# Norms spread by two float32r products instead of one fp32 product, two levels of the gated attention computed block by block, and products of ones at the program's start

## The chip, the cores and the metric

One core of one Trainium2 chip runs the whole program in one launch. The metric is the device time of an execution in microseconds (us); lower is better. The engines are named as in the profile: PE (TensorE, with PEld for its weight loads), DVE (VectorE), ACT (ScalarE), POOL (GpSimd), SP (SyncE).

## The reference

A decoder trunk of two layers on 512 tokens with 16 learned tokens ahead of them, so 528 columns; the model width is 1024, all in float32.

```python
# layer i:  x += 0.5*SwiGLU_a(RMSNorm(x)); x += Mixer_i(RMSNorm(x)); x += 0.5*SwiGLU_b(RMSNorm(x))
def rmsnorm(x, g):  # x * rsqrt(mean(x*x) + 1e-6) * g
def swiglu(x, w_in, w_out):      # d_ff = 2816
    gate, up = split(x @ w_in); return (silu(gate) * up) @ w_out
# mixer of layer 0: retention, 4 heads (dk 256, dv 512), rotary positions, a decay per head,
#   RMSNorm per head, gated by silu(g), output product
# mixer of layer 1: gated linear attention (GLA), 4 heads (dk 128, dv 256), a decay per key channel
#   and token, in exact form inside a chunk, RMSNorm per head, gated, output product
# at the end: final RMSNorm; the 16 learned tokens are dropped
```

So there are seven norms over the model width (two FFNs and a mixer per layer, and the final one), and one norm per head in each mixer.

## The kernel before

Activations lie with the channels on the partitions and the tokens in the columns; x stays on the core. A large product is made of three float32r products (`mm3`, L361 to L363): activations and weights are split into a high float32r part and the rest (`whi` by ACT at L139, `wlo` by DVE at L140), and high by high, rest by high and high by rest are added up in PSUM. The FFNs combine such products over halves of the matrices (`pf10g`, `Xf20o` and so on).

The RMSNorm of a stage is made by `enter(gcol, by, lag)`. While the stage before writes x, `scaled` (ACT, DVE L434) makes the two parts of x times the gain, and `squared` (ACT, DVE L442) adds the squares of the eight row groups of x up in `sqa_n`. Then `stats` runs: 1-column fp32 products with a column of ones sum the squares over the partitions, each for a block of tokens, and leave token sums on partitions (`st_n`, PE L468); `ms_n` (DVE L477) makes the mean; POOL raises it to -1/2 into `rc` (L479); DVE multiplies the identity by it, which gives diagonal blocks (`dg_n`, L481). One step of the stage later (`later`) `spread` multiplies the diagonals by a matrix of ones in fp32, which puts each token's factor on all partitions (`bc_n`, PE L488), and ACT copies it to `rb` (L489). The blocks of tokens are given by `by`: `BY_P` is 16 columns and four blocks of 128, `BY_JT` the same with the 16 at the end (on 16 partitions).

`rsqrt_rows` (L392) does the same for the norms of heads and the final one: `st` L401, `ms` L404, POOL L406, diagonal `dg` L408, spread `bc` L414. A retention head has six blocks of 88 tokens and two spreads of 264 columns (`ro`), a GLA head one of 512 (`go`), the end one of 256 (`fa`). What is made from `bc_ro` is the gated output `og`, split into `ogh` and `ogl` (DVE L390), which the output projection `po_r` takes.

The GLA computes scores inside a chunk by levels (`levels`): at level s, each token in the second half of a group of 2s is scored against the keys of the first half. `tile_scores` (L1395) makes, for each of two passes over pairs of heads, eight fp32 products of 128 keys by 64 queries into `lv`; most of the results aren't wanted, and DVE's `copy_predicated` (L1425) takes the wanted ones into `Pd` by a mask of level s. `advance` then multiplies decays into Q and K. Between levels, `filler` gives PE a step of other products.

The engines run their instructions in an order that a scheduler works out from the program and from priorities: `urgent()` puts what is inside it 300 steps ahead. Before the first FFN product is over, `plain_first` runs 96 float32r products that need no norm yet. Temporary tiles are taken from rings by tag; `hf` is a ring of two, which `dg`, `og` and the `hf` of the FFN share.

```python
def rsqrt_rows(sq, parts, width, name, finish):     # L392
    ...
    dg = tmp.tile([P, T], F32, tag="hf", name=f"dg_{name}")                 # L407
    V.tensor_tensor(dg[:w, :n]..., ident[:w, :w]..., r[:w, :nj]..., ALU.mult)
    def spread(q):
        nc.tensor.matmul(bc[:, :np_], lhsT=ones[:w, :], rhs=dg[:w, q * np_:(q + 1) * np_], start=True, stop=True)
```

Of the kernel before, what the change touches and what calls it, by code (L numbers as in the profile page):

```python
# [10 lines left out]
F32 = mybir.dt.float32  # L11
# [26 lines left out]

NJ = 5
# [5 lines left out]
BY_P = ((16, 128, 4, 512), (0, 128, 1, 16))  # L45
PW = 512
AHEAD = 4
HEAD_START = 300
# [149 lines left out]
def trunk(ctx, tc, a):  # L198
# [125 lines left out]
    ones = const.tile([P, P], F32, name="ones")  # L324
    V.memset(ones, 1.0)
# [65 lines left out]

    def rsqrt_rows(sq, parts, width, name, finish):  # L392
# [7 lines left out]
        for j in range(nj):  # L400
# [6 lines left out]
        dg = tmp.tile([P, T], F32, tag="hf", name=f"dg_{name}")  # L407
        V.tensor_tensor(dg[:w, :n].rearrange("p (j t) -> p j t", j=nj),  # L408
                        ident[:w, :w].unsqueeze(1).broadcast_to([w, nj, w]),
                        r[:w, :nj].unsqueeze(2).broadcast_to([w, nj, w]), ALU.mult)  # L410

        def spread(q):
            bc = bank(f"bc_{name}{q}")
            nc.tensor.matmul(bc[:, :np_], lhsT=ones[:w, :], rhs=dg[:w, q * np_:(q + 1) * np_], start=True, stop=True)  # L414
            finish(bc, q)
# [3 lines left out]
    def enter(gcol, by, lag=1):  # L419
# [42 lines left out]
        def stats():  # L462
# [11 lines left out]
            dg = tmp.tile([P, T], F32, tag="hf", name=f"dg_{name}")  # L474
            for (b0, w, nb, m), c in zip(by, cols):
# [4 lines left out]
                n = m // nb  # L480
                V.tensor_tensor(dg[:w, b0:b0 + m].rearrange("p (j t) -> p j t", j=nb),  # L481
                                ident[:w, :n].unsqueeze(1).broadcast_to([w, nb, n]),
                                r.unsqueeze(2).broadcast_to([w, nb, n]), ALU.mult)
# [791 lines left out]
    def gla(feed):  # L1275
        with tc.tile_pool(name="glap", bufs=1) as gp, psum_pool(2) as pp:
            other["pool"] = pp
            masks = gp.tile([P, 7, HP], I32, tag="masks", name="masks")
# [101 lines left out]
            def levels(p, filler):  # L1380
# [18 lines left out]

                pd_v = Pd.rearrange("p h (J i) -> p (h J) i", i=P)  # L1400
# [22 lines left out]
                while s <= 64:  # L1423
                    ps = tile_scores(f"lv{p}_{s}", s)
# [239 lines left out]
    feed = enter(G_F1, BY_P, 4)  # L1664
# [7 lines left out]
    retention(enter(G_F2, BY_P))  # L1672
    ffn("f2", 0, HALVES, G_F2, enter(G_F1 + 8, BY_P))
# [5 lines left out]
def _constants():  # L1679
# [14 lines left out]
    lmask = [((j >> n) % 2 == 0) & ((i >> n) == (j >> n) + 1) for n in range(7)]  # L1694
# [62 lines left out]
```

## Time and profile before

| what | us |
|---|---|
| median of three runs (lowest to highest) | 2105.49 (2105.16 to 2106.26) |
| the profiled execution: device time | 2106.07 |
| the profiled execution: span of the core | 2104.3 |
| PE busy | 2078.2 (99% of the span) |
| DVE busy | 1761.3 (84%) |
| ACT busy | 1165.0 (55%) |
| POOL busy | 195.9 (9%) |

The device time of the profiled execution is 1.8 us above its span, and 0.58 us above the median. Busy time of PE says that it had something in its pipeline, not that it was at its peak: what an event costs on PE is read from the distance between the starts of products around it.

### The profile page before, as it was taken

The numbers are of one execution on the slowest core, as the hardware profiler recorded it, in microseconds if no ns is written. First come the engines' busy times: TensorE is split into PE (matmuls) and PEld (weight loads), VectorE is DVE, ScalarE is ACT, GpSimd is POOL, SyncE is SP. The second block draws the span as 40 slices with busy tenths as digits, with TensorE's granted clock in tenths as the row PEclk, the third lists the DMA queues.
The fourth block names the chain that finished last, engine by engine and source line by source line (L and its number), as shares of the span: only waits on it lengthen the run. The fifth ranks groups of instructions, "written<-read, shape, count | busy, mean of one in ns | idle before, by whom it ended". The sixth has DMA issues, their size and how long they took to land.

```text
span 2104.3 us, 43710 instructions
## 1 busy us (share of the span) xinstructions
PE 2078.2 (99%) x16842; PEld 2051.9 (98%) x16842; DVE 1761.3 (84%) x3139; ACT 1165.0 (55%) x2250; POOL 195.9 (9%) x168
## 2 busy tenths in 40 slices
PE   8999999999999999999999999999999999999998
PEld 8999999999999999999999999999999999999998
DVE  8989889978686779988889998888775659998886
ACT  5656666554545455656665565666632335666664
POOL 1011111010101000111110011111000000111110
PEclk9999999999999999999999999999999999999999
DMA  7576777254544532776776476676512122586772
GB/s 219 154 191 159 191 183 192 88 151 121 152 121 126 142 100 66 183 194 155 197 182 163 114 177 184 167 196 170 146 61 68 57 73 67 136 221 168 188 181 71
DMA packets 171809, 309.12 MB, mean 147 GB/s; under 512 B 17104, under 2 KB 40016, under 8 KB 171600
## 3 DMA queue, kind: packets, MB, share of 16 engines
q1 hardware_dynamic: 131696, 231.20, 32.8%
q0 software_dynamic: 38896, 71.84, 21.1%
q10 hardware_dynamic: 1008, 3.29, 0.5%
q8 instruction: 132, 2.16, 0.4%
q14 instruction: 77, 0.63, 0.1%
HBM read 304.16 MB, written 2.10 MB: 146 GB/s over the span
## 4 chain that ended last, share of the span: by engine, by line
PE 92%; DVE 3%; ACT 2%; issue 1%; DMA 1%; POOL 0%; SPq 0%; DVEq 0%; POOLq 0%; ACTq 0%
PE po_r L361 1%; PE po_r L362 1%; PE po_r L363 1%; PE lv L1395 1%; PE Xf11o L361 1%; PE Xf20o L361 1%; PE Xf11o L363 1%; PE Xf20o L363 1%; PE Xf11o L362 1%; PE Xf20o L362 1%; PE Xf10o L361 1%; PE Xf10o L363 1%; PE Xf10o L362 1%; PE Xf11u L361 1%; PE Xf21o L361 1%
## 5 line engine op out<-in xcount | busy, mean ns | idle before, releaser
L139 ACT CAST whi<-raw 128x512 fp32r<-128x512 f32 (+1 forms) x886 | 524.1, 606 | 544.3 <-DVE raw L145 73.4
L140 DVE TENSOR_TENSOR wlo<-raw,whi 128x512 fp32r<-128x512 f32 (+1 forms) x886 | 580.0, 669 | 174.7 <-ACT whi L139 165.8
L139 ACT CAST whi<-pair 128x512 fp32r<-128x512 f32 (+1 forms) x290 | 174.8, 603 | 129.1 <-DVE pair L145 8.1
L140 DVE TENSOR_TENSOR wlo<-pair,whi 128x512 fp32r<-128x512 f32 (+1 forms) x290 | 192.3, 663 | 8.4 <-ACT whi L139 7.2
L112 POOL DMA_DIRECT2D pair<-in_f_in x75 | 91.1, 1215 | 767.1 <-DVE wlo L140 379.1
L112 POOL DMA_DIRECT2D pair<-in_f_out x48 | 58.1, 1210 | 414.2 <-DVE wlo L140 209.3
L145 DVE TENSOR_TENSOR raw<-pair,raw 128x512 f32<-128x512 f32 (+1 forms) x139 | 92.5, 665 | 2.6
L147 DVE TENSOR_TENSOR raw<-raw,raw 128x512 f32<-128x512 f32 (+1 forms) x139 | 92.4, 665 | 2.6
L361 PE MATMUL po_r<-ogh,whi 128*128 128x264 f32 x256 | 72.8, 284 | 1.3 <-DVE xa L873 1.3
L362 PE MATMUL po_r<-ogl,whi 128*128 128x264 f32 x256 | 72.8, 284 | 0.0
L363 PE MATMUL po_r<-ogh,wlo 128*128 128x264 f32 x256 | 72.5, 283 | 0.0
L112 POOL DMA_DIRECT2D pair<-in_ret_in x20 | 24.3, 1216 | 300.3 <-DMA pair<-in_ret_in 131.5
L361 PE MATMUL Xf11o<-hf,whi 128*128 128x264 f32 x176 | 51.0, 290 | 0.9 <-ACT whi L139 0.6
L361 PE MATMUL Xf20o<-hf,whi 128*128 128x264 f32 x176 | 51.0, 290 | 0.9 <-ACT whi L139 0.6
L361 PE MATMUL Xf10o<-hf,whi 128*128 128x264 f32 x176 | 50.9, 289 | 0.9 <-ACT whi L139 0.6
L362 PE MATMUL Xf11o<-hf,whi 128*128 128x264 f32 x176 | 50.1, 285 | 0.0
L362 PE MATMUL Xf20o<-hf,whi 128*128 128x264 f32 x176 | 50.1, 284 | 0.0
L362 PE MATMUL Xf10o<-hf,whi 128*128 128x264 f32 x176 | 50.1, 284 | 0.0
L363 PE MATMUL Xf20o<-hf,wlo 128*128 128x264 f32 x176 | 49.9, 284 | 0.0
L363 PE MATMUL Xf11o<-hf,wlo 128*128 128x264 f32 x176 | 49.9, 284 | 0.0
L363 PE MATMUL Xf10o<-hf,wlo 128*128 128x264 f32 x176 | 49.9, 284 | 0.0
L361 PEld LDWEIGHTS po_r<-ogh,whi 128*128 128x128 f32 x256 | 48.1, 188 | 1.7 <-DVE xa L873 1.7
(834 smaller groups left out, 8663.0 us busy)
## 6 DMA issues: line engine op xcount, KB each, us to landing
raw<-in_f_in SPq DMA_DIRECT2D x277, 256.0 KB, 4.4
pair<-in_f_in SPq DMA_DIRECT2D x150, 256.0 KB, 4.5
pair<-in_f_in POOLq DMA_DIRECT2D x75, 512.0 KB, 6.1
raw<-in_f_out SPq DMA_DIRECT2D x80, 256.0 KB, 3.7
raw<-in_ret_in SPq DMA_DIRECT2D x76, 256.0 KB, 3.3
raw<-in_f_out SPq DMA_DIRECT2D x72, 192.0 KB, 3.0
raw<-in_gla_in SPq DMA_DIRECT2D x50, 256.0 KB, 2.8
pair<-in_f_out SPq DMA_DIRECT2D x48, 256.0 KB, 3.8
```

Of the source, the lines that this page charges most:

```text
L112: nc.gpsimd.dma_start(t, aps[2].unsqueeze(1).broadcast_to([P, 2, n]), accum_op=ALU.add)
L139: self.nc.scalar.copy(hi[:, :n], raw)
L140: V.tensor_sub(lo[:, :n], raw, hi[:, :n].bitcast(F32))
L145: V.tensor_add(s2, self.tiles[c][:, 1], self.tiles[c, "a11"])
L147: V.tensor_add(raw, raw, s2)
L361: nc.tensor.matmul(ps, lhsT=lh, rhs=rh, start=start, stop=False, **kw)
L362: nc.tensor.matmul(ps, lhsT=lh, rhs=rl, start=False, stop=False, **kw)
L363: nc.tensor.matmul(ps, lhsT=ll, rhs=rh, start=False, stop=stop, **kw)
L1395: nc.tensor.matmul(ps[:, j, J * P:J * P + n], lhsT=Kt[:, j, J * P:(J + 1) * P], rhs=q, start=(J == 0), stop=(J == 3), skip_group_check=True)
```

## The change

1. `diagonals` takes the factor apart into its float32r high part and the rest (two small DVE instructions, a CAST L411 and a subtraction L412) and makes two diagonals, `dgh` and `dgl` (L414), both in the ring `hf`. `spread_rows` (L420) adds up two float32r products with ones. It takes the place of the one fp32 product in `enter` and in `rsqrt_rows`.
2. In `enter` for the inputs of the first FFN (`G_F1`), of layer 0's second FFN (`G_F2`) and of layer 1's first FFN (`G_F1 + 8`) the blocks of tokens are `BY_6`: six blocks of 88 in one group, so one mean, one power and one diagonal instruction instead of two each, and the spread in two pieces of 264 columns. The inputs of the retention, of the GLA and of the last FFN keep blocks of 128.
3. GLA levels 32 and 64 are computed by `block_scores`: for each group of tokens and each tile, one product of s keys by s queries (16 of 32x32 at level 32, 8 of 64x64 at level 64, per pass), and ACT copies the results into `Pd`, two copies at level 32 and one at level 64. `copy_predicated` goes at these levels.
4. Ten float32r products of ones (`warm`, 128x512, L336) stand ahead of the first product, into a PSUM tile that isn't read.

```diff
-    ones = const.tile([P, P], F32, name="ones")
-    V.memset(ones, 1.0)
+    ones_r = const.tile([P, P], F32R, name="ones")
+    V.memset(ones_r.bitcast(F32), 1.0)
+    ones = ones_r.bitcast(F32)
+    warm = acc.tile([P, 2, 512], F32, tag="acc", name="warm")[:, 0, :]...
+    for _ in range(WARM):                                    # WARM = 10
+        nc.tensor.matmul(warm, lhsT=ones_r, rhs=ones_r.unsqueeze(1).broadcast_to([P, 4, P]), start=True, stop=True)
+    def parts_of(name):
+        return [tmp.tile([P, T], F32R, tag="hf", name=f"dg{i}_{name}") for i in "hl"]
+    def diagonals(dg, name, r, w, c0, n):
+        nj = r.shape[1]
+        m = n // nj
+        rr = tmp.tile([P, 2, 8], F32R, tag="rr", name=f"rr_{name}")
+        V.tensor_copy(rr[:w, 0, :nj], r)
+        V.tensor_sub(rr[:w, 1, :nj], r, rr[:w, 0, :nj].bitcast(F32))
+        for i, d in enumerate(dg):
+            V.tensor_tensor(d[:w, c0:c0 + n].rearrange("p (j t) -> p j t", j=nj),
+                            ident[:w, :m].unsqueeze(1).broadcast_to([w, nj, m]),
+                            rr[:w, i, :nj].bitcast(F32).unsqueeze(2).broadcast_to([w, nj, m]), ALU.mult)
+    def spread_rows(ps, dg, w, c0):
+        for i, d in enumerate(dg):
+            nc.tensor.matmul(ps, lhsT=ones_r[:w, :], rhs=d[:w, c0:c0 + ps.shape[1]], start=(i == 0), stop=(i == 1))
...
+BY_6 = ((0, 88, 6, 528),)
             def spread():
                 for b0, w, nb, m in by:
-                    bc = bank(f"bc_{name}_{b0}")
-                    nc.tensor.matmul(bc[:, :m], lhsT=ones[:w, :], rhs=dg[:w, b0:b0 + m], start=True, stop=True)
-                    S.copy(rb[:, b0:b0 + m], bc[:, :m])
+                    n = m if m <= 512 else m // 2
+                    for c0 in range(b0, b0 + m, n):
+                        bc = bank(f"bc_{name}_{c0}")
+                        spread_rows(bc[:, :n], dg, w, c0)
+                        S.copy(rb[:, c0:c0 + n], bc[:, :n])
...
+                def block_scores(name, s):
+                    ps = acc_tile(name)
+                    blocks = range(P // (2 * s))
+                    for j in range(2):
+                        for n in blocks:
+                            k0 = 2 * s * n
+                            for J in range(4):
+                                nc.tensor.matmul(ps[k0:k0 + s, j, J * P:J * P + s],
+                                                 lhsT=Kt[:, j, J * P + k0:J * P + k0 + s],
+                                                 rhs=Qt[:, j, J * P + k0 + s:J * P + k0 + 2 * s],
+                                                 start=(J == 0), stop=(J == 3), skip_group_check=True)
+                    for n in blocks:
+                        k0 = 2 * s * n
+                        S.copy(pd_v[k0:k0 + s, :, k0 + s:k0 + 2 * s],
+                               ps.rearrange("p h (J i) -> p (h J) i", i=P)[k0:k0 + s, :, :s])
...
                 while s <= 64:
+                    if s >= BLOCKS:                          # BLOCKS = 32
+                        block_scores(f"lv{p}_{s}", s)
+                        tot = advance(s, tot)
+                        filler()
+                        s *= 2
+                        continue
...
-    feed = enter(G_F1, BY_P, 4)
+    feed = enter(G_F1, BY_6, 4)
-    retention(enter(G_F2, BY_P))
-    ffn("f2", 0, HALVES, G_F2, enter(G_F1 + 8, BY_P))
+    retention(enter(G_F2, BY_6))
+    ffn("f2", 0, HALVES, G_F2, enter(G_F1 + 8, BY_6))
```

The change moves instructions at three places that matter below. The first is DVE at the end of the retention, between its last sums of squares (`sqa_n`) and the next FFN's input, where `BY_6` is used; `wlo` is the vector half of a weight split. Before:

```order
L442 TENSOR_TENSOR sqa_n_4926<-sqa_n_4926,sq_n_7_10420 128x528
L140 TENSOR_TENSOR wlo_10570<-raw_10220,whi_10569 128x512
L477 TENSOR_SCALAR ms_n_10489<-st_n_10482 128x4
L477 TENSOR_SCALAR ms_n_10493<-st_n_10482 128x1
L481 TENSOR_TENSOR dg_n_10488<-ident,rc 128x512
L481 TENSOR_TENSOR dg_n_10488<-ident,rc 128x16
L140 TENSOR_TENSOR wlo_10576<-raw_10286,whi_10575 128x512
```

With the change:

```order
L470 TENSOR_TENSOR sqa_n_4941<-sqa_n_4941,sq_n_7_10474 128x528
L146 TENSOR_TENSOR wlo_10628<-raw_10274,whi_10627 128x512
L505 TENSOR_SCALAR ms_n_10545<-st_n_10536 88x6
L411 CAST rr_n_10548<-rc 88x6
L412 TENSOR_TENSOR rr_n_10548<-rc,rr_n_10548 88x6
L414 TENSOR_TENSOR dgh_n_10543<-ident,rr_n_10548 88x528
L414 TENSOR_TENSOR dgl_n_10544<-ident,rr_n_10548 88x528
L146 TENSOR_TENSOR wlo_10634<-raw_10340,whi_10633 128x512
```

Two pairs of small and large instructions have become a mean, two small ones and two diagonals, in one run between the same two `wlo`.

The second is DVE at the retention's input, where `BY_JT` stays. Before:

```order
L477 TENSOR_SCALAR ms_n_5008<-st_n_5001 128x4
L477 TENSOR_SCALAR ms_n_5012<-st_n_5001 16x1
L140 TENSOR_TENSOR wlo_4986<-raw_4841,whi_4985 128x512
L481 TENSOR_TENSOR dg_n_5007<-ident,rc 128x512
L481 TENSOR_TENSOR dg_n_5007<-ident,rc 16x16
L140 TENSOR_TENSOR wlo_4992<-raw_4859,whi_4991 128x512
L140 TENSOR_TENSOR wlo_5041<-raw_4883,whi_5040 128x512
```

With the change:

```order
L146 TENSOR_TENSOR wlo_5001<-raw_4856,whi_5000 128x512
L411 CAST rr_n_5027<-rc 128x4
L411 CAST rr_n_5035<-rc 16x1
L146 TENSOR_TENSOR wlo_5007<-raw_4874,whi_5006 128x512
L412 TENSOR_TENSOR rr_n_5027<-rc,rr_n_5027 128x4
L414 TENSOR_TENSOR dgh_n_5022<-ident,rr_n_5027 128x512
L414 TENSOR_TENSOR dgl_n_5023<-ident,rr_n_5027 128x512
L412 TENSOR_TENSOR rr_n_5035<-rc,rr_n_5035 16x1
L414 TENSOR_TENSOR dgh_n_5022<-ident,rr_n_5035 16x16
L146 TENSOR_TENSOR wlo_5065<-raw_4898,whi_5064 128x512
L414 TENSOR_TENSOR dgl_n_5023<-ident,rr_n_5035 16x16
L146 TENSOR_TENSOR wlo_5113<-raw_4922,whi_5112 128x512
```

The CAST of the 16-token group stands ahead of the diagonals of the 512 tokens, and two `wlo` more lie between the CASTs and the last diagonal.

The third is PE at that same place, where the products `pq` run ahead of the norm. Before:

```order
L361 MATMUL pq_4942<-uha,whi_4855 128x264
L362 MATMUL pq_4942<-ula,whi_4855 128x264
L363 MATMUL pq_4942<-uha,wlo_4856 128x264
L488 MATMUL bc_n_0_5046<-dg_n_5007,ones 128x512
L488 MATMUL bc_n_512_5049<-dg_n_5007,ones 128x16
L361 MATMUL pq_5061<-uha,whi_4879 128x264
```

With the change:

```order
L372 MATMUL pq_5087<-uha,whi_4894 128x264
L420 MATMUL bc_n_0_5070<-dgh_n_5022,ones 128x512
L373 MATMUL pq_5087<-ula,whi_4894 128x264
L374 MATMUL pq_5087<-uha,wlo_4895 128x264
L372 MATMUL pq_5087<-uha,whi_4894 128x264
L420 MATMUL bc_n_0_5070<-dgl_n_5023,ones 128x512
L420 MATMUL bc_n_512_5074<-dgh_n_5022,ones 128x16
L373 MATMUL pq_5087<-ula,whi_4894 128x264
L374 MATMUL pq_5087<-uha,wlo_4895 128x264
L372 MATMUL pq_5087<-uha,whi_4894 128x264
L373 MATMUL pq_5087<-ula,whi_4894 128x264
L420 MATMUL bc_n_512_5074<-dgl_n_5023,ones 128x16
```

The two spreads stood together; now other products lie between their halves.

## Rows read from the trace of the kernel before

**Rows 1.** The profile page: the line of part 1 on busy time (share of the span, instructions), and the first line of part 4, the shares by engine of the chain that ended last.

```profile
PE 2078.2 (99%) x16842; PEld 2051.9 (98%) x16842; DVE 1761.3 (84%) x3139; ACT 1165.0 (55%) x2250; POOL 195.9 (9%) x168
PE 92%; DVE 3%; ACT 2%; issue 1%; DMA 1%; POOL 0%; SPq 0%; DVEq 0%; POOLq 0%; ACTq 0%
```

**Rows 2.** The waits of PE, grouped: engine, line, what was waited for, us in total, times, longest. One row out of the list.

```profile
PE bc_ro L414 <- DVE dg_ro L408: 1.5, 2, 0.9
```

**Rows 3.** The timeline of PE at the start of the program, from the first product to the first statistics (columns of every timeline below: start in us, length in us, engine, line, operation, output<-inputs, shapes, count, idle time before it and its releaser).

```profile
5.46 0.59 PE L361 MATMUL pf10g<-uha,whi 128*128 128x264 f32 x1 [5.46 <-ACT whi L139]
...
7.44 0.42 PE L362 MATMUL pf10u<-ula,whi 128*128 128x264 f32 x1
7.66 0.42 PE L363 MATMUL pf10u<-uha,wlo 128*128 128x264 f32 x1
...
12.14 0.28 PE L363 MATMUL pf10g<-uha,wlo 128*128 128x264 f32 x1
12.26 0.29 PE L361 MATMUL pf10u<-uha,whi 128*128 128x264 f32 x1
...
20.17 0.28 PE L363 MATMUL pf10u<-uha,wlo 128*128 128x264 f32 x1
20.61 1.28 PE L468 MATMUL st_n<-ones,sqa_n 128*128 128x1 f32 x10 [0.16 <-DVE sqa_n L442]
```

**Rows 4.** Busy time of the engines in two stretches of the start; the columns are stretch, us, then busy (instructions) of PE, PEld, DVE, ACT, POOL, the granted clock of TensorE, DMA share, GB/s.

```profile
8.00:11.50 3.50, 3.50 (x18) 3.50 (x17) 3.23 (x5) 3.50 (x7) 0.00 (x0) 1.00 1.05 406
12.00:20.00 8.00, 8.00 (x68) 8.00 (x67) 8.00 (x14) 7.53 (x14) 2.16 (x2) 1.00 1.07 379
```

**Rows 5.** The timeline of DVE just ahead of the first statistics.

```profile
19.25 0.69 DVE L140 TENSOR_TENSOR wlo<-raw,whi 128x512 fp32r<-128x512 f32 x1
19.86 0.70 DVE L442 TENSOR_TENSOR sqa_n<-sqa_n,sq_n 128x528 f32<-128x528 f32 x1
```

**Rows 6.** The timeline of PE around spreads: in pairs, the spread (or the group of spreads) and the second float32r product behind it. First the input of layer 0's second FFN (512 and 16 columns), then that of the retention (512 columns from 128 rows, 16 from 16 rows), then a GLA head (512 columns), then the last retention head (264 columns from 88 rows; a fp32 product is recorded twice).

```profile
801.43 1.15 PE L488 MATMUL bc_n<-dg_n,ones 128*128 128x512 f32 x4
802.63 0.28 PE L361 MATMUL pf20u<-uha,whi 128*128 128x264 f32 x1
...
366.74 1.41 PE L488 MATMUL bc_n<-dg_n,ones 128*128 128x512 f32 x4
368.30 0.28 PE L362 MATMUL pq<-ula,whi 128*128 128x264 f32 x1
...
1615.25 1.02 PE L414 MATMUL bc_go<-dg_go,ones 128*128 128x512 f32 x2
1616.23 0.29 PE L362 MATMUL pg_gq<-ula,whi 128*128 128x272 f32 x1
...
757.06 0.61 PE L414 MATMUL bc_ro<-dg_ro,ones 88*128 88x264 f32 x2
757.63 0.29 PE L362 MATMUL QZrg<-ula,whi 128*128 128x264 f32 x1
```

**Rows 7.** The timeline of PE around column statistics, in pairs as before: five of 128 columns at layer 0's second FFN, then six of 88 of a retention head.

```profile
797.74 1.18 PE L468 MATMUL st_n<-ones,sqa_n 128*128 128x1 f32 x10
798.99 0.28 PE L362 MATMUL pf20g<-ula,whi 128*128 128x264 f32 x1
...
666.22 1.03 PE L401 MATMUL st_ro<-ones,osq 128*88 128x1 f32 x12
667.32 0.28 PE L362 MATMUL Xrqkq<-rtl,whi 128*128 128x264 f32 x1
```

**Rows 8.** The timeline of PE around one GLA level of eight 128x64 products (each recorded twice, x16), with the second product behind it; and two neighbouring float32r products of 16 rows into 16 columns in the retention.

```profile
1556.34 1.89 PE L1395 MATMUL lv<-Q,K 128*128 128x64 f32 x16
1558.25 0.28 PE L362 MATMUL gv<-ula,whi 128*128 128x264 f32 x1
...
417.80 0.17 PE L361 MATMUL sc<-q,k 128*16 128x16 f32 x1 [0.30 <-DVE pl L390]
417.83 0.17 PE L362 MATMUL sc<-q,k 128*16 128x16 f32 x1
```

**Rows 9.** The timeline of PE, two neighbouring float32r products with 512 columns in the GLA.

```profile
1598.59 0.40 PE L362 MATMUL go<-PF,v 128*128 128x512 f32 x1
1598.82 0.39 PE L363 MATMUL go<-PF,v 128*128 128x512 f32 x1
```

**Rows 10.** The chain from statistics to spread: the power of a retention head on POOL (min, median and max of four, in ns, with first and last start; 88x6); then power (POOL) and diagonal (DVE) of layer 0's second FFN, whose spread is the first row of rows 6; then power, diagonal and spread (PE) of layer 1's GLA input. The power and the diagonal of 512 columns and of 16 are recorded together (x2).

```profile
L406 POOL TENSOR_TENSOR r_ro<-ms_ro,half_neg x4: 1342/1686/1731, 454.8 to 752.9; 88x6 f32<-88x6 f32 x4
...
799.21 1.54 POOL L479 TENSOR_TENSOR rc<-ms_n,half_neg 128x4 f32<-128x4 f32 x2 [20.89 <-DVE ms_n L477]
800.27 0.78 DVE L481 TENSOR_TENSOR dg_n<-ident,rc 128x512 f32<-128x512 f32 x2 [1.09 <-POOL rc L479]
...
1496.10 1.56 POOL L479 TENSOR_TENSOR rc<-ms_n,half_neg 128x4 f32<-128x4 f32 x2 [5.80 <-DVE ms_n L477]
1497.17 0.78 DVE L481 TENSOR_TENSOR dg_n<-ident,rc 128x512 f32<-128x512 f32 x2 [0.95 <-POOL rc L479]
1498.17 1.15 PE L488 MATMUL bc_n<-dg_n,ones 128*128 128x512 f32 x4
```

**Rows 11.** The last vector half (DVE) of the first retention head's gated output, and the product of the output projection (PE) that takes it.

```profile
468.81 0.42 DVE L390 TENSOR_TENSOR ogl<-og,ogh 128x264 fp32r<-128x264 f32 x1
...
471.30 0.29 PE L362 MATMUL po_r<-ogl,whi 128*128 128x264 f32 x1
```

More of the change, by code (lines that the diff above doesn't have):

```diff
@@ L37 @@
 RH, RDV = 4, 512
+BLOCKS = 32
+NMASK = 5
 NJ = 5
@@ L45 @@
 BY_P = ((16, 128, 4, 512), (0, 128, 1, 16))
+BY_6 = ((0, 88, 6, 528),)
 PW = 512
 AHEAD = 4
+WARM = 10
 HEAD_START = 300
@@ L323, in trunk @@
     nc.sync.dma_start(causal, a["tri"][1])
-    ones = const.tile([P, P], F32, name="ones")
-    V.memset(ones, 1.0)
+    ones_r = const.tile([P, P], F32R, name="ones")
+    V.memset(ones_r.bitcast(F32), 1.0)
+    ones = ones_r.bitcast(F32)
+    warm = acc.tile([P, 2, 512], F32, tag="acc", name="warm")[:, 0, :].rearrange("p (n c) -> p n c", c=P)
+    for _ in range(WARM):
+        nc.tensor.matmul(warm, lhsT=ones_r, rhs=ones_r.unsqueeze(1).broadcast_to([P, 4, P]), start=True, stop=True)
     half_neg = const.tile([P, 8], F32, name="half_neg")
@@ L406, in rsqrt_rows @@
         G.tensor_tensor(r[:w, :nj], ms[:w, :nj], half_neg[:w, :nj], ALU.pow)
[L407 to L410, printed above, removed]
+        dg = parts_of(name)
+        diagonals(dg, name, r[:w, :nj], w, 0, nj * w)
         def spread(q):
             bc = bank(f"bc_{name}{q}")
-            nc.tensor.matmul(bc[:, :np_], lhsT=ones[:w, :], rhs=dg[:w, q * np_:(q + 1) * np_], start=True, stop=True)
+            spread_rows(bc[:, :np_], dg, w, q * np_)
             finish(bc, q)
@@ L473, in stats @@
                 col += nb
-            dg = tmp.tile([P, T], F32, tag="hf", name=f"dg_{name}")
+            dg = parts_of(name)
             for (b0, w, nb, m), c in zip(by, cols):
@@ L479, in stats @@
                 G.tensor_tensor(r, ms[:w, :nb], half_neg[:w, :nb], ALU.pow)
[L480 to L483, printed above, removed]
+                diagonals(dg, f"{name}{c}", r, w, b0, m)
             def spread():
                 for b0, w, nb, m in by:
-                    bc = bank(f"bc_{name}_{b0}")
-                    nc.tensor.matmul(bc[:, :m], lhsT=ones[:w, :], rhs=dg[:w, b0:b0 + m], start=True, stop=True)
-                    S.copy(rb[:, b0:b0 + m], bc[:, :m])
+                    n = m if m <= 512 else m // 2
[3 more added lines that the diff above has]
+                        S.copy(rb[:, c0:c0 + n], bc[:, :n])
             later(1, spread)
@@ L1277, in gla @@
             other["pool"] = pp
-            masks = gp.tile([P, 7, HP], I32, tag="masks", name="masks")
+            masks = gp.tile([P, NMASK, HP], I32, tag="masks", name="masks")
             nc.sync.dma_start(masks, a["lmask"])
@@ L1693, in _constants @@
     j, i = np.arange(P)[:, None], np.arange(P)[None, :]
-    lmask = [((j >> n) % 2 == 0) & ((i >> n) == (j >> n) + 1) for n in range(7)]
+    lmask = [((j >> n) % 2 == 0) & ((i >> n) == (j >> n) + 1) for n in range(NMASK)]
     lmask = np.stack([m[:, (i[0] >> n) % 2 == 1] for n, m in enumerate(lmask)], 1).astype(np.int32)
```

## The prediction

> **What bounds the kernel.** I read the page first: PE is busy for 2078 of 2104 us and carries 92% of the chain that ended last; DVE is second [rows 1]. So the end moves by what PE is spared or made to wait, and a change on DVE counts only where PE stands still for it. The list of PE's waits, read next, has such places, among them two of the retention heads' spreads, 1.5 us together [rows 2]. Then I read PE's timeline around each thing that the change touches. There float32r products with 264 columns start 0.12 us apart [rows 3] and those with 512 columns 0.23 us apart [rows 9]. What an event costs PE is the start of the second float32r product behind it, less its own start, less 0.12. All "costs" below are made so.
>
> The sum is made against the profiled execution (2106.07 us, span 2104.3); the median is 0.58 below, and I move the sum to the median. A measurement of this kernel can tell about 0.2%, 4.2 us, from no change.
>
> **The spreads alone.** A fp32 spread of 512 columns costs 0.86, one of 264 columns 0.45, 512 with 16 behind 1.08, and with 16 from 16 rows 1.44 [rows 6]. Two float32r products cost 2 x 0.23 or 2 x 0.12. So where the diagonals are there in time:
> - four GLA heads: 4 x (0.86 - 0.46) = -1.6. The work around is long enough to hide one more diagonal; I count it all.
> - four retention heads, two spreads each: 2 x (0.45 - 0.24) = -0.42 each, so -1.7. Heads 2 and 3 already waited for the diagonal [rows 2]; now the second diagonal comes 0.8 later, but the order puts other products of the head ahead and between the halves. I take -1.4 for the four, bounds -2.6 (the waits go as well) and +1.5 (each head waits 0.8 for its second half).
>
> **The norms over the width.** Here the diagonal is on a short path: power on POOL, diagonal on DVE, spread. At layer 0's second FFN the power starts at 799.21, the first diagonal at 800.27, 1.06 later, and PE comes to the spread at 801.43 [rows 6, 10]. With `BY_6` there is one power of 88x6, as in a retention head: 1.34 to 1.73 [rows 10], so 0.3 to 0.6 later. CAST and subtraction add some 0.16 (from the 0.08 by which the 16-column diagonal prolongs the recorded pair over a single one of 0.70 [rows 5, 10]), and each large diagonal takes about 0.62 of DVE, the distance of such instructions [rows 5]. `dgl` is then ready near 799.21 + 1.5 + 0.16 + 1.24 + 0.06 = 802.2. PE is there at 801.3, as six column sums of 88 cost 0.98 against 1.13 for five of 128 [rows 7], and has one product to do first: a wait of about 0.75 to 0.9. The spread falls from 1.08 to 0.48, the sums save 0.15. Net +0.15 each at the inputs of layer 0's second and layer 1's first FFN, +0.3 together; bounds -0.75 (no wait) and +0.8 (a weight split of 0.61 slips ahead of `dgl`) each.
>
> At the first FFN the same holds with the same path; there the order leaves more products between, and I take -0.15.
>
> At the retention's input (`BY_JT`) the second CAST needs the second power, and it stands ahead of the diagonals; one `wlo` stands between the CASTs and the rest. That is 0.5 (the second power, from 1.56 for the pair less 1.07 to the diagonal [rows 10]) + 0.61 + 0.16 + 0.62 = 1.9 later for `dgl`, against three other products, 0.4, and nothing saved up before. And 16 rows of weights cost 1.44 - 1.08 = 0.36 more [rows 6], which two separate small products may pay twice: 0.46 + 0.1 + 0.72 for 1.44. I take +0.75; bounds -0.8 (all in time) and +1.6.
>
> At the GLA's input (`BY_P`) CAST also waits for the second power, until 1497.66; then two small ones, `dgh` 0.62, `dgl` 0.62, and the 16 columns: `dgl` is ready near 1499.1, where PE arrives at 1498.17 [rows 10]. 0.9 of wait, 0.3 more for the last 16 columns, 0.5 for the products, less 1.08: +0.65; bounds -0.5 and +1.2. At the last FFN's input (512 columns alone, like a GLA head but on the short path) -0.15, bounds -0.4 and +0.9. At the final norm the saving of 0.2 stands against a longer path near the end: +0.15, bounds -0.3 and +0.9.
>
> **GLA levels 32 and 64.** A level of eight 128x64 products costs 1.79 [rows 8], 0.22 a product. No fp32 product of 32x32 is in the trace. Its bounds: two passes at the 0.025 of the narrow float32r products [rows 8], so 16 x 0.05 = 0.8 a level, and the same 0.22 as the wide one, 3.6. I take 1.2, nearer the narrow end, because rows and columns are a quarter of the wide product's; for level 64, half as many keys and the same queries, 1.1, between 0.9 and 1.79. Two passes: 2 x (0.59 + 0.69) = -2.6; bounds -3.8 and +3.6. `copy_predicated` leaves DVE; ACT, at 55% [rows 1], takes three short copies a pass, with the filler's products to hide them.
>
> By a rule of the Trainium skill, "TensorEngine Tiling (Array Packing)", section "Key Properties", changing the tiling mode drains TensorE, which speaks against the small blocks. If each of the four levels paid for that once what the 16-row product does (0.36), the levels would save 1.2 in place of 2.6 and the sum would be 1.4 worse. The nearest row only shows that small weights from 16 rows cost extra, not why.
>
> **Products of ones at the start.** The first product waits 5.46 us for its weights; then products of 264 columns start 0.22 apart (1.2 GHz), and from about 12 us 0.12 apart (2.4 GHz) [rows 3], while the granted clock is recorded as 1.00 in both stretches [rows 4]. About 29 products lie in the slow stretch, so at most 29 x 0.10 = 2.9 us could be won. But PE then comes to `st_n`, which needs the eighth square sum: DVE ends it at 19.86 + 0.70 = 20.56 and PE starts at 20.61 [rows 3, 5], and DVE is busy for all of 12 to 20 us [rows 4] with the same instructions as before. PE stands in order behind it, so the gain becomes a wait of 2.3 us at `st_n`. The ten products lie in idle time, 1.1 to 5.4 us. I count 0, bounds -0.3 and +0.3.
>
> **The rest.** In the first retention head the score products have moved ahead of other ones, one group onto a DVE half (`pl`) which it waited for already 0.30 [rows 8]: +0.45, bounds 0 and +1. Some 12 large diagonals more are about 8 us of DVE work, hidden where DVE isn't the waited-for engine.
>
> **Sum.** -1.6 - 1.4 - 0.15 + 0.3 + 0.75 + 0.65 - 0.15 + 0.15 - 2.6 + 0 + 0.45 = -3.6. From 2106.07 that is 2102.5, and 2101.9 at the median: -0.17%.
>
> **Rivals.**
> - *The diagonals are in time* (chance 0.22). If the power is at the short end and the order's other products cover `dgl`, the norms over the width each keep what the spread saves: -0.75 twice, -0.5 at the first, -0.5 at each mixer input, -0.4 at the last FFN. That is -3.9 in place of +1.4, a sum of -8.9; with half of them in time -6 to -7, so about 2099. For it: the retention's order has such cover. Against it: before, the spread came 0.4 behind the diagonal's end at best [rows 6, 10].
> - *The products of ones pay* (0.08). Then the first sums don't hold PE, and 2.3 to 2.9 us come off: 2099.3. The Trainium skill, "TensorE: Matmul & The Clock Gate", section "Why this matters for your kernels", advises warming the array up with products before the real ones, which would be this result. Rows 3 show that the slow stretch is real, rows 5 that it isn't what the sums wait for.
> - *The clock falls back* (0.06). A PE that waits 2.3 us at `st_n` returns to 0.22 spacing behind it, about as long as at the start: +3, so about 2105.
> - *Late halves on DVE* (0.08, slower). In each tight spread a `wlo` of 0.61 stands ahead of `dgl` by arrival, so that twelve places lose about 0.9 more: +11. In a retention head `og` is later by that too; the last `ogl` ends at 469.23 and `po_r` takes it at 471.30 [rows 11], so the 2.1 us of slack hold until the spread is over 2 us late, and then PE waits for the rest. It gives 2101.9 + 11 = 2113, with half of the places 2107. It decides when waits of PE on `dgl` pass 1 us in most places; DVE at 84% speaks for it, the order (the two diagonals mostly stand together) against.
> - *The small blocks cost as much as the wide products* (0.06): the levels become +3.6 in place of -2.6: 2108.
>
> The forecast has 0.50.
>
> **How the numbers follow.** The forecast's own terms have a spread of some 2 us: 2100 to 2104. The first two rivals reach down to about 2098, the third and halves of the last two up to about 2106. Range 2098 to 2106; it leaves out the whole of the two slower cases and the lower half of the first rival. Faster by over 0.2% means below 2101.28: 0.40 of the forecast's half, most of the first two rivals: 0.20 + 0.19 + 0.07 = 0.46. Slower means over 2109.7: most of the late halves and a little of the small blocks, 0.07. Same is the rest, 0.47. Though the chances are close, the likeliest single time is the sum's, 2101.9.
>
> **What would show it.** In the profile after: no distance of 0.22 behind the first product, and a wait of about 2.3 us of `st_n` for `sqa_n`; waits of `bc_n` for a diagonal of 0.5 to 1 us at layer 0's second FFN, layer 1's first and both mixers, none at `bc_go`; GLA levels of about 1.2 and 1.1; `bc_go` at 0.46. It is wrong if `bc_n` waits nowhere, if `st_n` starts ahead of 20 us, or if a level of 32 takes over 1.8.

## The result and the profile after

| | before | changed |
|---|---|---|
| median of seven runs | 2106.26 us (2105.16 to 2107.71) | 2114.01 us (2111.37 to 2114.76) |
| the profiled execution: time, span | 2106.07, 2104.3 | 2111.37, 2109.6 |

The change is slower: ratio 1.0035, 95% interval 1.0023 to 1.0046; the medians lie 7.8 us apart. I forecast 2101.9 and a range to 2106. The profiled execution of the changed kernel is the fastest of its seven, 2.6 us below their median, so it shows 5.3 of the 7.8 us.

The page of the changed kernel, its line of busy times and its chain; they answer to [rows 1]:

```profile
PE 2078.8 (99%) x16890; PEld 2051.7 (97%) x16890; DVE 1770.3 (84%) x3180; ACT 1168.2 (55%) x2256; POOL 195.3 (9%) x165
...
PE 90%; DVE 6%; ACT 2%; issue 1%; POOL 0%; DMA 0%; SPq 0%; DVEq 0%; POOLq 0%; ACTq 0%
```

PE is busy 0.6 us longer than before, while the span has grown by 5.3 and DVE's share of the chain has gone from 3% to 6%: PE waits more, and for DVE. The list of PE's waits in the changed kernel (waited for, us, times, longest; rows that bear on nothing below are left out):

```profile
PE st_n L496 <- DVE sqa_n L470: 2.3, 1, 2.3
PE po_r L374 <- DVE wlo L146: 2.3, 1, 2.3
PE po_r L372 <- DVE xa L900: 2.1, 2, 1.1
...
PE sc L372 <- DVE pl L401: 1.6, 5, 0.5
PE bc_ro L420 <- DVE dgh_ro L414: 1.3, 2, 1.0
PE bc_n L420 <- DVE dgh_n L414: 1.2, 2, 1.0
PE po_r L372 <- ACT ogh L400: 1.1, 1, 1.1
...
PE bc_n L420 <- DVE dgl_n L414: 0.5, 2, 0.2
```

Before, the list had one row of `po_r` of this size:

```profile
PE po_r L361 <- DVE xa L873: 1.3, 2, 1.1
```

The column sums, `po_r` for `wlo` and `ogh`, and the norms' spreads are new among the large ones. Three of them, 2.3, 2.3 and 1.1 us, are single waits at places where nothing was edited or where I had booked a gain.

The start (timeline of PE, the first product, the first column sums and two products behind them; it answers to [rows 3]) and busy times there (columns as in [rows 4]: PE, PEld, DVE, ACT, POOL, then the granted clock):

```profile
5.58 0.39 PE L372 MATMUL pf10g<-uha,whi 128*128 128x264 f32 x1 [0.29 <-ACT whi L145]
...
20.60 0.55 PE L496 MATMUL st_n<-ones,sqa_n 128*88 128x1 f32 x5 [2.26 <-DVE sqa_n L470]
...
22.67 0.42 PE L374 MATMUL pf10g<-uha,wlo 128*128 128x264 f32 x1
22.89 0.42 PE L372 MATMUL pf10g<-uha,whi 128*128 128x264 f32 x1
```

```profile
15.00:20.00 5.00, 3.34 (x28) 3.13 (x26) 5.00 (x9) 4.25 (x8) 1.49 (x2) 1.00 1.07 379
22.00:25.00 3.00, 3.00 (x15) 3.00 (x15) 2.33 (x6) 0.00 (x0) 1.72 (x1) 0.50 1.06 298
26.00:30.00 4.00, 4.00 (x35) 4.00 (x34) 2.35 (x5) 3.31 (x6) 0.00 (x0) 1.00 1.06 333
```

PE is 2.1 us ahead at 15 us, stands 2.26 us at `st_n` for the square sum, as forecast, and is DVE-bound there (5.00 of 5.00). Behind the wait the clock is granted at 0.50 and 16 products start 0.22 us apart, the lower of the two levels; at 0.12 they would have taken 1.6 us less.

Spreads (PE; of the retention's input, of layer 0's second FFN, of the GLA's input, of a GLA head; they answer to [rows 6]):

```profile
369.64 0.50 PE L420 MATMUL bc_n<-dgh_n,ones 128*128 128x512 f32 x1 [0.96 <-DVE dgh_n L414]
...
807.77 0.39 PE L420 MATMUL bc_n<-dgh_n,ones 88*128 88x264 f32 x1
808.38 0.39 PE L420 MATMUL bc_n<-dgl_n,ones 88*128 88x264 f32 x1 [0.23 <-DVE dgl_n L414]
808.61 0.28 PE L420 MATMUL bc_n<-dgh_n,ones 88*128 88x264 f32 x1
808.73 0.29 PE L420 MATMUL bc_n<-dgl_n,ones 88*128 88x264 f32 x1
808.85 0.29 PE L374 MATMUL pf20u<-uha,wlo 128*128 128x264 f32 x1
...
1505.55 0.50 PE L420 MATMUL bc_n<-dgh_n,ones 128*128 128x512 f32 x1 [0.25 <-DVE dgh_n L414]
1506.15 0.50 PE L420 MATMUL bc_n<-dgl_n,ones 128*128 128x512 f32 x1
...
1604.16 0.40 PE L420 MATMUL bc_go<-dgh_go,ones 128*128 128x512 f32 x1
1604.40 0.39 PE L420 MATMUL bc_go<-dgl_go,ones 128*128 128x512 f32 x1
1604.63 0.40 PE L372 MATMUL go<-PF,v 128*128 128x512 f32 x1
```

At the retention's input PE waited 0.96 for the first diagonal. At the second FFN it waited 0.23 between the halves, and 808.85 less 807.77 is 1.08, as much as before; with what the sums save, this norm comes out even (forecast +0.15). At the GLA's input the halves stand 0.6 apart, one DVE diagonal, and the place costs 0.8 (forecast 0.65). In the GLA head two products follow without a gap, 0.47 in place of 0.86, as summed.

Level 32 (PE; it answers to the first pair of [rows 8]):

```profile
1564.21 0.90 PE L1435 MATMUL lv<-Q,K 128*32 128x32 f32 x32
...
1565.27 0.28 PE L373 MATMUL gv<-ula,whi 128*128 128x264 f32 x1
```

1565.27 - 1564.21 - 0.12 = 0.94 against 1.79; I had taken 1.2. Level 64 costs 1.10, as I took. The four places together give 2.1 us in e4's profile below, against the 2.6 of my sum; the product ahead of each small level stands 0.21 before it in place of 0.12.

For the rest I matched the products of two profiles one by one and read how the distance between their starts grows. Over the program, changed less before: +0.7 at 50 us; about +0.5 between 60 and 70 us, in the first FFN, where PE waits 0.4 each for `gf` (DVE) and `suf10g` (ACT); +0.8 at the retention's input and +0.65 at its first scores; nothing in heads 0 and 1, +0.9 in head 2, +1.9 in head 3; +0.8 at the GLA's input; -3.5 in the GLA; and, not at any place, about 0.5 us over the rest of the first FFN and 1.2 over the others. The step at 60 to 70 us is in the profiles of e1, e3, e15 and e17 below too, which have the norms' part.

### The profile page after: what moved, and what is told of

It reads as the page before. It is cut to its first block, busy times and chain, and to the rows that moved or that the text cites. A ratio compares the mean times of both kernels' runs of the same rounds, so it can differ in the third digit from the quotient of the medians.

```text
span 2109.6 us, 43845 instructions
## 1 busy us (share of the span) xinstructions
PE 2078.8 (99%) x16890; PEld 2051.7 (97%) x16890; DVE 1770.3 (84%) x3180; ACT 1168.2 (55%) x2256; POOL 195.3 (9%) x165
## 4 chain that ended last, share of the span: by engine, by line
PE 90%; DVE 6%; ACT 2%; issue 1%; POOL 0%; DMA 0%; SPq 0%; DVEq 0%; POOLq 0%; ACTq 0%
PE po_r L373 1%; PE po_r L374 1%; PE po_r L372 1%; DVE wlo L146 1%; PE Xf11o L372 1%; PE Xf10o L372 1%; PE Xf20o L372 1%; PE Xf11o L374 1%; PE Xf11o L373 1%; PE Xf10o L374 1%; PE Xf20o L374 1%; PE Xf20o L373 1%; PE Xf10o L373 1%; PE lv L1422 1%; PE Xf11u L372 1%
## 5 line engine op out<-in xcount | busy, mean ns | idle before, releaser
L374 PEld LDWEIGHTS po_r<-ogh,wlo 128*128 128x128 f32 x256 | 48.2, 188 | 2.5 <-DVE wlo L146 2.5
```

The lines of the kernel that those rows point to most:

```text
L374: nc.tensor.matmul(ps, lhsT=ll, rhs=rh, start=False, stop=stop, **kw)
```

## The experiments

Each is compared in five rounds with the kernel before on the same chip (its median there 2106.3 to 2106.8); "+" is slower. Theory **R**: the second diagonal on DVE makes work of the retention late, and PE waits at the output projection. **S**: such waits come from the order that the scheduler makes. **W**: the products of ones cost more than they give. **D**, later **P**: products that nothing touched take longer, by executions (D) or by placement (P).

**e1**, the changed kernel with `WARM = 0`:

```diff
-    for _ in range(WARM):
-        nc.tensor.matmul(warm, lhsT=ones_r, ...)
```

> The changed kernel without the ten products of ones; all else as changed. Theory W (the products of ones cost time: PE comes 2.1 us earlier to the column sums, stands 2.26 us for the last square sum, and the clock is then granted at 0.50 for 3.4 us, which the trace of the changed kernel shows as 1.5 us of wider spacing): 1.0 to 1.5 us less than the changed kernel, no wait over 0.3 us at the first column sums and no granted clock under 1.00 behind them. Rival (the start is a wash, as predicted): the same time within 0.5 us.

2112.0 us, ratio 1.0023 (1.0013 to 1.0033): 2.0 us less than the changed kernel by the medians, 2.3 by their distances to before. At 50 us its products are 0.8 us ahead of the changed kernel's, with no low clock there. But in its profile the clock falls to 0.50 behind the 2.3-us wait in head 2. W holds in sign; the exact size isn't told from one profile.

**e2**, before with the two-part spread in the retention heads alone; **e3**, before with it and `BY_6` in `enter` alone; **e4**, before with `block_scores` alone:

```diff
 e2  rsqrt_rows for ro:  +dgh, dgl, two float32r products
 e3  enter:              +dgh, dgl, two float32r products; +BY_6 at G_F1, G_F2, G_F1 + 8
 e4  levels 32 and 64:   +block_scores
```

> The kernel before with the two-part spread in the retention heads alone. Theory R (the loss lies in the retention: the second diagonal and its two small instructions sit on DVE's short path between the power and the gated output, DVE comes later to a weight half, an ogh or an ogl that the output projection needs, and PE waits there): slower than before by 2.5 to 4 us, waits of po_r for wlo, ogh or ogl of 1 to 4 us in total. Rival S (the scheduler's other order of the whole retention, which comes from the norms and the scores, makes those waits; the heads' spread alone saves what I summed): faster by about 1.4 us. Rival D (a drift over all products, which the trace shows as some 0.15% more per product): no change here beyond that.

> The kernel before with the two-part spread in the seven-minus-one norms over the width that go through enter, and the six blocks of 88 in three of them; heads, final norm, GLA levels and start as before. Theory R: about +1.5 to +2 us, as summed (+1.4) plus the disturbed score products at the retention's input, waits of bc_n for dgh_n or dgl_n of 1 to 2 us. Rival S: +4 or more, with waits at po_r. Rival D: +3 us spread over all products.

> The kernel before with GLA levels 32 and 64 block by block, and nothing else. Theory: 2.4 to 2.8 us less than before, as the trace of the changed kernel shows a loss of 1.2 us per level pair at two places. Rival (masks on DVE were what the GLA waited for): over 4 us less. Rival D: no gain to be seen, within 1 us.

e2: +5.3 us (1.0027; 1.0017 to 1.0036). e3: +4.9 (1.0024; 1.0016 to 1.0033). e4: -1.6 (0.9993; 0.9984 to 1.0001). So the heads, on which I had booked -1.4, lose, with waits of `po_r` for `wlo` of 2.3 and for `ogh` of 1.0. But e2's profile shows some 2.8 us at the heads and e3's some 2.4 at the norms; the rest grows evenly, in e2 and e3 and not in e4. And in e2 the clock falls at the start too, without products of ones, behind a wait of 1.5.

**e5**, the changed kernel with the sums one step later:

```diff
-    feed = enter(G_F1, BY_6, 4)
+    feed = enter(G_F1, BY_6, 5)
```

> The changed kernel with the first column sums one step later in the program (a lag of 5 instead of 4, which puts 19 more float32r products, 2.3 us, ahead of them). Theory W (the products of ones do make PE's start faster, and all of it and more is lost by the wait of 2.26 us for the last square sum and the lower clock behind it): 3 to 3.5 us less than the changed kernel, about 1 to 1.5 less than it without the products of ones; no wait over 0.3 us at the first sums and a granted clock of 1.00 behind them. Rival (the clock falls for another reason, such as the fp32 sums themselves): the granted clock still drops behind the sums and the time stays within 0.7 us of the changed kernel.

2113.3 us, 1.0031 (1.0019 to 1.0042): no cure. The sums no longer wait, but the spread behind them does (2.2 us for `dgh_n`), and the clock falls there. My theory of the cure was wrong: it isn't the sums' place, DVE is what the start waits for.

**e6**, before with one float32r diagonal and one product in the heads (the low part of their factors is left out):

```diff
-        return [tmp.tile([P, T], F32R, tag="hf", name=f"dg{i}_{name}") for i in "hl"]
+        return [tmp.tile([P, T], F32R, tag="hf", name=f"dg{i}_{name}") for i in "h"]
...
-        V.tensor_sub(rr[:w, 1, :nj], r, rr[:w, 0, :nj].bitcast(F32))
```

> The kernel before with the retention heads' factors rounded to float32r: one diagonal and one float32r product per spread. It leaves out the low part of these factors. Against the kernel with both parts in the heads alone it lacks one subtraction, one diagonal of 0.62 us on DVE and one product per spread; the CAST stays. Theory R (the second diagonal on DVE's path makes the waits at the output projection): waits of po_r for wlo, ogh and ogl under 1 us in total, 1.5 to 2.5 us less than the kernel before. Rival S (it is the order of instructions that the scheduler makes out of any change there, with weight halves and the gated output in another order): waits of po_r of over 2 us stay, and the time is 0 to 3 us above before.

2107.2, 1.0000 (0.9991 to 1.0008). Its waits of PE (rows for `po_r` and `bc_ro`):

```profile
PE po_r L369 <- DVE xa L908: 1.9, 3, 0.8
...
PE bc_ro L428 <- DVE dgh_ro L419: 1.7, 2, 0.9
```

No wait for `wlo`, `ogh` or `ogl` is left, and its products win 1.5 us between 430 and 800 us; the median is no lower: in the profile the even growth (below, 1.4 us) and a wait of 0.8 for `suf21o` in the last FFN take it back. R's condition holds in the profile, its time doesn't.

**e7**, before with the levels and the two-part spread of the GLA heads alone; **e8**, the same with the products of ones and the sums one step later.

> The kernel before with GLA levels 32 and 64 block by block and the two-part spread in the four GLA heads alone: the parts with nothing on DVE's short path. Theory: the levels gave 1.6 us; the GLA heads give 1.2 to 1.6 more as summed, so 2.8 to 3.2 us less than before, and no wait of PE at bc_go. Rival (in the GLA heads too the second diagonal makes later work late): no more than the levels alone.

> The same parts, and the ten products of ones with the first column sums one step later (lag 5), all spreads over the width in fp32 as before. Theory W: 1.5 to 2.2 us less than with the two GLA parts alone, so 4.5 to 5.5 us less than before. Rival (the start is bounded by DVE's work and not by PE): the same as the two GLA parts alone, within 0.5 us.

e7: 2105.6, 0.9994 (0.9985 to 1.0003). In its profile the GLA gains 3.5 us, but 2.0 have grown before it. e8: 2107.4, 0.9999 (0.9990 to 1.0008): 1.8 more than e7, where I had expected less; the two intervals overlap. The first spread in its profile:

```profile
28.10 2.08 PE L429 MATMUL bc_n<-dg_n,ones 128*128 128x512 f32 x4 [1.92 <-DVE dg_n L415]
```

It waits 1.92 us for its diagonal in place of the sums, and behind it the clock is granted at 0.50 again, for twice as long as in the changed kernel. So at the start DVE bounds, and an earlier PE only gets a longer wait.

**e9**, the kernel before once more, for a second profile; **e10** and **e11**, before with the two-part spread in head 2, or head 3, alone; **e12**, as e2 with `dgl` made by POOL:

```diff
-            V.tensor_tensor(d[:w, ...
+            (V, G)[i].tensor_tensor(d[:w, ...
```

> The kernel before, unchanged, with a profile of its own: what two executions of one kernel differ by. Theory D (a slow drift between executions): between the same products of the two profiles the distance grows by 0.1 to 0.2% in the FFNs, up to 2 us over the program, and the start differs by up to 1 us; the median is that of before within 0.05%. Rival: the two profiles agree within 0.3 us all along, and the drift in the other profiles belongs to their edits.

> The kernel before with the two-part spread in the third retention head (h2) alone. Theory R: the wait of po_r for a weight half wlo (2.3 us) comes back, +0.9 net, and up to 1.5 us more where the granted clock falls behind it: 0.9 to 2.4 us slower than before. Rival S (such a wait comes only from the order that all four heads' edits make together): no wait of po_r over 1 us, and 0 to 1 us faster.

> The kernel before with the two-part spread in the last retention head (h3) alone. Theory R: the waits of po_r for ogh and ogl (1.0 and 0.4 us) come back and the last head loses 1.5 to 2 us. Rival S: these waits come from what the earlier heads made late; here 0 to 0.7 us faster.

> The two-part spread in the four retention heads alone, with the low part's diagonal made by POOL instead of DVE. Theory R (DVE's 0.62 us per head is what makes the later waits): the waits of po_r for wlo, ogh and ogl go, and the time falls by 1 to 4 us against the same with both diagonals on DVE, less what PE then waits for POOL's diagonal, which I put at 1 to 3 us long. Rival S: the waits at po_r stay as they are.

e9: 2107.35, 1.0000 (0.9991 to 1.0009). Its products differ from the first profile's by up to 1.6 us at the start (its clock falls behind a wait of 1.3) and 0.8 at one wait in the retention, and elsewhere by under 0.3: the even growth is no matter of executions, and D falls. e10: +3.6 (1.0016; 1.0007 to 1.0025). e11: +4.9 (1.0024; 1.0014 to 1.0033), 2.0 of it in head 3; in its profile another 1.6 stand in the next FFN, where the clock falls behind a wait of 0.9. Both bring their waits back alone. Both also have the small tile whose price e13 gives, 1.9 us; less that, e10 lies in R's range. In e10, windows ahead of, behind, and after the wait at 685 us:

```profile
680.00:685.00 5.00, 3.00 (x25) 2.79 (x23) 4.69 (x9) 2.88 (x6) 1.23 (x1) 1.00 0.69 150
686.10:689.40 3.30, 3.30 (x18) 3.30 (x17) 3.30 (x7) 0.39 (x1) 0.00 (x0) 0.50 0.47 135
690.00:695.00 5.00, 5.00 (x43) 5.00 (x42) 3.79 (x7) 2.47 (x5) 0.00 (x0) 1.00 0.32 112
```

The granted clock is 0.50 behind it, which costs 1.5 more. e12: +3.2 (1.0014; 1.0005 to 1.0023). Its waits at `po_r` and the heads' spreads:

```profile
PE po_r L369 <- DVE xa L909: 2.5, 3, 1.0
PE bc_ro L429 <- POOL dgl_ro L420: 2.2, 4, 0.5
```

The waits for `wlo`, `ogh` and `ogl` are gone, and PE waits 2.2 us for POOL's diagonal instead: 1.38 us each against 0.70 on DVE. Against before it is 2.1 us better than e2; R expected 1 to 4.

**e13** and **e14**, before with a tile that is never read; **e15**, the changed kernel, **e16**, e7's parts, with the two parts in the ring `r`, so that nothing moves:

```diff
 e13, e14
+    pad = tmp.tile([P, 16], F32, tag="rr", name="pad")      # e14: 32
+    V.memset(pad, 0.0)
 e15, e16
-        rr = tmp.tile([P, 2, 8], F32R, tag="rr", name=f"rr_{name}")
+        rr = [tmp.tile([P, 8], F32R, tag="r", name=f"rr{i}_{name}") for i in "hl"]
...
-        r = tmp.tile([P, 8], F32, tag="r", name=f"r_{name}")
+        r = ms if ... else tmp.tile([P, 8], F32, tag="r", name=f"r_{name}")
```

The second pair of lines writes the power over the mean where the two-part spread is used, so e15 and e16 change a little more than the place; e13 and e14 add the tile and its one zeroing alone.

> The kernel before with one more small tile of 128 bytes per partition, which is zeroed once and never read, at the place where the changed kernel keeps the two parts of a factor: every tile behind it, weights and activations, lies 128 bytes further on. Not one other instruction changes. Theory P (placement: each float32r product takes some 0.2 ns longer for it, which is the growing distance in every profile that has the tile and in none that hasn't): 1.5 to 3 us slower than before, growing by 0.1 to 0.2% over the FFNs. Rival (the growth comes from the edits' extra work on DVE): the time of before within 0.5 us, and no growth.

> The same with 256 bytes. Theory P as a matter of the alignment: another growth than with 128 bytes, between none and twice as much. Rival (any shift costs): the same growth as with 128 bytes.

> The changed kernel with the parts of a factor kept in a ring that exists already, so that no tile behind it is shifted by 128 bytes; the same products, diagonals, levels and products of ones. Theory P: no growth over the FFNs, 1.5 to 3 us less than the changed kernel, so about 2111 to 2112.5. Rival: the changed kernel's time within 0.5 us.

> Levels 32 and 64 block by block and the two-part spread in the GLA heads alone, unshifted. Theory P: the GLA's gain of 3.5 us shows in full: 2103 to 2104, against 2105.6 shifted. Rival: 2105 to 2106 as before.

e13: 2108.67, +1.9, 1.0011 (1.0002 to 1.0020). e14: 2107.1, 1.0001 (0.9993 to 1.0010). e15: 2109.9, 1.0013 (1.0005 to 1.0022), where the changed kernel had 1.0035; that is 4.1 us less, and P had expected 1.5 to 3. In the two profiles, apart from the clock behind head 2, about 2.3 are seen; the rest is not explained. e16: **2103.4, 0.9984 (0.9976 to 0.9993)**, faster than both kernels. How much the distance to the first profile of before grows, in us, over 950 us of FFN products that no edit touches (90 to 360, 850 to 1140, 1165 to 1485 and 1780 to 1850, as products of the kernel before):

| shifted by 128 bytes | | not, or by 256 | |
|---|---|---|---|
| changed kernel | 1.54 | e15, the same unshifted | 0.20 |
| e13, the tile alone | 1.45 | e14, 256 bytes | 0.24 |
| e7 | 1.36 | e16, the same unshifted | 0.29 |
| e3 | 1.47 | e17, the same unshifted | 0.30 |
| e2 | 1.38 | e18, the same unshifted | -0.08 |
| | | e9, before again | 0.14 |
| | | e4 | 0.01 |

P holds: of the two shifts tried, 128 bytes cost and 256 don't. By what mechanism is open.

**e17** and **e18**, e3 and e2 unshifted (the edit of e15).

> The kernel before with the two-part spread and the blocks of 88 in the norms over the width alone (as e3), the two parts in an existing ring, so nothing shifts. Theory P: e3's 4.9 us fall to the 2 to 3 us that its trace shows at the places of the edit: about 0.9 at the retention's input, 0.8 at its first scores, 0.8 at the GLA's input. Rival: 4 us or more.

> The kernel before with the two-part spread in the retention heads alone (as e2), unshifted. Theory R and P together: e2's 5.3 us fall to 2.5 to 4 us, the waits of the output projection that e2's trace shows and, in some executions, the lower clock behind the longest of them. Rival: 5 us as in e2.

e17: +2.6 (1.0011; 1.0002 to 1.0020). e18: +2.9 (1.0013; 1.0004 to 1.0022). e18 shows head 2 at its clearest. Before, the first weight half that its output projection needs (DVE) and the product that takes it (PE):

```profile
678.69 0.68 DVE L140 TENSOR_TENSOR wlo<-raw,whi 128x512 fp32r<-128x512 f32 x1
```

```profile
682.60 0.28 PE L363 MATMUL po_r<-ogh,wlo 128*128 128x264 f32 x1
```

The same in e18 (DVE, then PE):

```profile
680.26 0.70 DVE L1076 TENSOR_TENSOR raq<-rtq,ropeq 128x528 f32<-128x528 f32 x1
680.88 0.70 DVE L1078 TENSOR_TENSOR rbq<-rtq,ropeq 128x528 f32<-128x528 f32 x1
681.50 0.70 DVE L1077 TENSOR_TENSOR rtq<-rtq,ropeq 128x528 f32<-128x528 f32 x1
682.12 0.70 DVE L1079 TENSOR_TENSOR raq<-raq,rbq 128x528 f32<-128x528 f32 x1
682.74 0.70 DVE L1083 TENSOR_TENSOR rtq<-rtq,ropeq 128x528 f32<-128x528 f32 x1
683.36 0.68 DVE L146 TENSOR_TENSOR wlo<-raw,whi 128x512 fp32r<-128x512 f32 x1
```

```profile
684.10 0.47 PE L371 MATMUL po_r<-ogh,wlo 128*128 128x264 f32 x1 [2.30 <-DVE wlo L146]
```

PE would have been there at 681.80; DVE has five steps of the rotary product, 3.1 us, ahead of the weight half, which before stood ahead of all of them. The changed kernel has the same five at 684.13 to 687.23, where its weight half starts. They stand there in every kernel whose head 2 has both diagonals on DVE, and the wait of 2.3 is in each; with one diagonal (e6) or the second on POOL (e12) the weight half is ahead of them, and there is no such wait. In head 3 the order changes in the same way. What `ogh` is made of is `gs`; before, DVE made it straight behind an `ogl`:

```profile
770.99 0.43 DVE L390 TENSOR_TENSOR ogl<-gs,ogh 128x264 fp32r<-128x264 f32 x1
771.34 1.14 DVE L1259 TENSOR_TENSOR gs<-gs,ob 128x528 f32<-128x528 f32 x2
```

In the changed kernel two weight halves stand between (DVE, then PE):

```profile
776.26 0.43 DVE L401 TENSOR_TENSOR ogl<-gs,ogh 128x264 fp32r<-128x264 f32 x1 [0.92 <-ACT ogh L400]
776.61 1.29 DVE L146 TENSOR_TENSOR wlo<-raw,whi 128x512 fp32r<-128x512 f32 x2
777.81 1.05 DVE L1286 TENSOR_TENSOR gs<-gs,ob 128x528 f32<-128x528 f32 x2
```

```profile
779.23 0.51 PE L372 MATMUL po_r<-ogh,whi 128*128 128x264 f32 x2 [1.08 <-ACT ogh L400]
```

So R and S are each half right: the second diagonal on DVE is the occasion, and what PE waits for in head 2 is the order that the scheduler then writes, not the 0.62 us. Why it writes that order (presumably it expects the gated output later) isn't shown, and no run has both diagonals on DVE with the old order.

## Why the prediction was wrong

It went to the other side. The parts, as each alone measured:

| part | forecast | measured |
|---|---|---|
| levels and GLA heads | -2.6, -1.6 | -3.3 (e16) |
| norms through `enter`, with the scores of the first head | +1.4, +0.45 | +2.6 (e17) |
| retention heads | -1.4 | +2.9 (e18) |
| products of ones | 0 | +2.0 (changed kernel less e1) |
| a small tile that shifts all behind it | not there | +1.9 (e13) |

They add up to 6.1 of the 7.8 us, each uncertain by some 2 us; the final norm lost about 0.4 in the profile. The granted clock of whole runs points at the rest. Of the changed kernel's seven runs, the two with a mean of 0.998, the profiled one among them, took 2111.4 and 2111.9 us, and the five with 0.997 took 2113.1 to 2114.8. In e15 three runs at 0.999 took 2107.7 to 2107.9, the eight at 0.998 or 0.997 took 2109.7 to 2111.9, and its profile, at 0.997, has the clock at 0.50 twice, at the start and in head 2. So the median of the changed kernel probably has the lower clock in head 2 as well, which its profile has not; none of the five has a profile to show it.

- **The heads' term failed.** I priced the spread where it stands, and there I was right: when the wait of head 2 begins, e18's products are 1.0 us ahead of those of before. The measured +2.9 is beyond my bound of +1.5 too. My step "the 2.1 us of slack hold", written in the last rival but one, looked at the last `ogl` alone and took the rest of DVE's order for unchanged. In head 2 it is a weight half that comes late, by 2.3 us of wait, in head 3 `ogh`, by 1.1 in the changed kernel. About 1.5 us of e18's loss is the lower clock behind the wait of head 2, as in e10. The order of DVE's instructions could have shown the step: the five rotary steps stand ahead of the weight half. I read the order at the edit, not up to the next place that PE takes something from that queue.
- **The start's mechanism was right**, down to the wait (2.3 forecast, 2.26 measured), and its price wrong: I counted 0 and gave the lower clock behind the wait a chance of 0.06. The array was at the higher level earlier (0.12 spacing from about 6.7 us, against 12 us before), and the wait with the lower clock behind it took more than that. The Trainium skill, "TensorE: Matmul & The Clock Gate", section "Why this matters for your kernels", advises to warm up with products first; it says so of benchmarks. In this kernel such products lose in both comparisons, by 2.0 (changed kernel less e1) and 1.8 us (e8 less e7).
- **The placement was in no rival.** Nothing in the trace of before could show it; the diff does show a new tile in a pool ahead of the weights' own.
- **The norms were right in kind**, short by 0.7. Of the waits of 0.5 to 1 us that I expected at four places, the retention's input has one, of 0.96; the GLA's input and the two FFNs have 0.23 to 0.25. The step in the first FFN at 60 to 70 us, 0.45 in e17, was in no term of mine, and the first scores of the retention lost 0.65 to 0.9 against my 0.45.
- **The GLA was right in kind**, 0.9 short of the sum. By the rule of the Trainium skill, "TensorEngine Tiling (Array Packing)", section "Key Properties", a change of tiling mode drains TensorE; in my forecast that would have taken 1.4 back. The profile shows 0.09 more than usual ahead of each small level, and level 32 as a whole cost less than I took; if there is a drain, it is no more than that and what lies inside the 0.94.
- Of the rivals, "late halves on DVE" came nearest in time (2107 to 2113), but its mechanism, a `wlo` ahead of each `dgl`, isn't what the traces show. The first rival's sum is off by 0.5: its terms give -3.4, not -3.9.

## What to carry to other kernels

When a scheduler writes each engine's order, price an edit not only where it stands but up to the next thing that the bounding engine takes from each queue it touches; the order can be read before a run. Work that makes the bounding engine early is worth nothing in front of a wait for another engine, and here the clock fell behind the longer wait. A new small tile can shift the large ones: measure that shift alone before blaming the edit. Here a ring that existed already, or 256 bytes in place of 128, avoided its cost.

## What was not expected of the hardware

- The same float32r products took about 0.15% longer in sum (1.4 us in 950) with every tile behind a point moved by 128 bytes per partition, and not by 256.
- In 12 of the 20 profiles the granted clock fell to 0.50 for a few us behind a wait of PE of about 0.9 to 2.3 us, mostly at the start or in the retention, and cost some 1.5 us, more where it lasted longer (e8); behind other waits of the same 2.3 us it stayed at 1.00 (the changed kernel's head 2). It fell in one of the two profiles of the kernel before as well. What decides is open.
